# Layer 2's depthwise convolution on pairs of tokens: half the matmul passes, sixteen small spread transfers instead of four, and a gather behind them

## The chip, the cores and the metric

The kernel runs on the 8 cores of one Trainium2 chip. Each core has a tensor engine (PE, with its weight loads shown as PEld; it writes its results to a memory called PSUM), a vector engine (DVE), a scalar engine (ACT), GpSimd (POOL) and a sync engine (SP), which here does nothing but issue transfers. All transfers of a core run on its 16 DMA engines. The metric is the device time of the slowest core, in microseconds (us).

A program on all cores has a second, slower state, in which one die is granted a lower tensor clock.

Line numbers such as L921 are lines of that kernel's own source. Because the change inserts lines, the same work has other numbers afterwards:

| work in layer 2 | before | after |
|---|---|---|
| input projections (one helper for all layers) | L461 | L461 |
| gated product into G (DVE) | L882 | L893 |
| convolution (PE) | L921 | L937 |
| evacuation of the convolution, that is its copy out of PSUM, with bias (ACT) | L926 | L945 |
| square for the variance (ACT) | L928 | L958 |
| statistics (PE) | L937 | L966 |
| normalisation and SiLU (ACT) | L985 | L1015 |
| issue of any transfer (one helper) | L131 | L130 |

## The reference, cut to what matters

Four layers, one token mixer each. The change is in layer 2 alone, a Conformer convolution module: a gated product, a causal depthwise convolution with 31 taps over 2048 channels, a LayerNorm over the channels, SiLU.

```python
h = rms_norm(x, g_norm[i]) * (1.0 + scale) + shift
...
    a, ag, z = jnp.split(jnp.einsum('bsd,de->bse', h, w_in_c), 3, axis=-1)
    glu = a * jax.nn.sigmoid(ag)
    ext, conv_c_new = with_history(glu, hist_c, CCONV_W - 1)      # 30 earlier rows
    y = causal_depthwise_conv(ext, w_conv_c) + b_conv_c           # 31 taps, each channel for itself
    y = jax.nn.silu(layer_norm(y, ln_c_g, ln_c_b))                # statistics over all 2048 channels
    out = jnp.einsum('bse,ed->bsd', y * jax.nn.silu(z), w_out_c)
x = x + gate * out
```

Because the LayerNorm needs sums over all channels, nothing of the normalisation can start before the statistics of the last channel tile.

## The kernel before

Each core works on about 2 x 1,056 tokens in two groups (g = 0 and 1). In layer 2, 2048 channels make 16 tiles of 128, and a software-pipelined loop runs over them. In iteration i the tensor engine does the two projections of tile i, the convolution of tile i-2 and the statistics of tile i-3; the sync engine then spreads tile i:

```python
for i in range(16):
    ...                      # every second i: wait for the two weight tiles of i and i+1
    front(i, tl)             # 2 projections (PE), sigmoid (ACT), product into G (DVE)
    if i % 2 == 1:
        for sp in specs: release(sp)
        hook(i // 2)         # frees weight buffers; the next weight loads are issued by GpSimd
    if i >= 2: conv(i - 2)
    if i >= 3: stats(i - 3)
    spread(i)
zmm(0)                       # projections of the gate path z begin to be mixed in
conv(14); stats(13)
zmm(1)
conv(15); stats(14)
zmm(2)
stats(15)
variance()
...                          # then centre, normalise, multiply, limited largely by VectorE
```

A depthwise convolution has no sum over channels, so the kernel makes one for the tensor engine. Four transfers a tile copy G so that each block R[:, j] holds 32 channels at 4 token offsets: 128 rows. A weight matrix of 128 rows by 32 columns, zero except where row and column belong to the same channel, then applies 4 taps at once; 8 such passes (b) make 32 taps. Four blocks j run side by side on four column groups of the array.

```python
def spread(c):
    R, G = v3(tb(RB[ci], 4480), 4), tb(GB[ci], GW)
    for j in range(4):
        g = G[32 * j:32 * j + 32, CO:CO + RW]
        s.dma("sp", "gr%d_%d" % (ci, j), R[:, j, 0:RW],
              bass.AP(g.tensor, g.offset, [list(g.ap[0]), [1, 4], [1, RW]]), ...)
    ...                                           # DVE builds the masked weights wd

def conv(c):
    for b in range(8):
        for n in range(3):                        # 3 x 352 (or 362) tokens
            for j in range(4):                    # 4 column groups
                h.matmul(PSB[32*j:32*j+32, 3*sl + n, 0:WC], lhsT=wd[:, b, j, :],
                         rhs=R[:, j, 4*b + n*WC : 4*b + (n+1)*WC], start=(b == 0), stop=(b == 7), ...)
    ...                                           # ACT evacuates with the bias straight into ysT,
    ...                                           # then squares ysT into SQ
def stats(c):                                     # column sums of ysT and of SQ, accumulated over c
    ...
```

G, R, wd and SQ have two buffers each, chosen by the tile's parity.

## Time and profile before

The time before is 2298.93 us, the median of 3 runs (2295.59 to 2299.51). The profiled execution has a span of 2292.5 us.

| | kernel before |
|---|---|
| TensorE busy, share of the span | 2180.7 us, 95% |
| mean granted TensorE clock | 0.985 on the slowest core |
| one iteration of the channel loop | 11.47 us (group 0), 11.38 us (group 1) |
| of it: two projections / convolution / statistics | 7.47 / 3.71 / 0.29 us (group 0) |
| idle TensorE inside the loop | none |

These are lines of the profile page of the kernel before: busy time per engine, the chain of work that ended last (by engine, then by line), the group of the convolution, and the two kinds of spread transfer (size of each, median us from issue to landing).

```profile
PE 2180.7 (95%) x16875; PEld 1355.2 (59%) x16875; DVE 1046.1 (46%) x1482; ACT 638.4 (28%) x758; POOL 192.4 (8%) x336
...
PE 88%; DVE 5%; DMA 4%; ACT 2%; issue 1%; POOL 0%; DVEq 0%; SPq 0%; ACTq 0%; POOLq 0%
...
L921 PE MATMUL ps<-tmp 128*32 128x352 bf16 (+1 forms) x3072 | 122.9, 315 | 0.0
...
tmp<-tmp SPq DMA_DIRECT2D x64, 278.5 KB, 5.9
tmp<-tmp SPq DMA_DIRECT2D x64, 271.0 KB, 5.8
```

The number after the last bar of a group is the idle time of the engine just before its instructions: 0.0 for the convolution. It never waits.

This is the chain of waits of the kernel before in three iterations of the loop (start us, duration us, what):

```profile
1245.77 7.46 PE ps L461 x48
1253.24 3.71 PE ps L921 x96
1256.95 0.29 PE ps L937 x6
1257.24 7.47 PE ps L461 x48
1264.71 3.71 PE ps L921 x96
1268.42 0.29 PE ps L937 x6
1268.72 7.47 PE ps L461 x48
1276.18 3.71 PE ps L921 x96
```

Projections, convolution, statistics, then at once the next projections: the chain stays on the tensor engine. The convolution's 96 matmuls are 24 sets of four, so one set takes 3.71 / 24 = 155 ns.

This is the table by stretch for most of the same loop in the kernel before (busy us and instructions of each engine, granted clock, DMA share, GB/s):

```profile
1250.00:1385.00 135.00, 135.00 (x1785) 86.03 (x1783) 35.02 (x48) 38.61 (x36) 6.40 (x12) 1.00 0.64 145
```

The tensor engine is busy for all of 135 us at full clock; VectorE and ScalarE are busy for about a quarter.

### The profile page before, as it was taken

To read this page: it belongs to the slowest core of one execution; us is meant where nothing else is said; L and a number is where in the kernel's file an instruction comes from. 1 tells how busy PE (TensorE), PEld (TensorE's weight loads), DVE (VectorE), ACT (ScalarE), POOL (GpSimd) and SP (SyncE) were. 2 spreads that over 40 slices of the span, in tenths; PEclk is the share of its full clock that TensorE was granted. 3 is DMA by queue.
4 is the path that set the end of the run, shared out by engine and by line. 5 is a ranking of instruction groups with operands and counts; after the bars stand their busy time and mean duration, and the time that the engine had idled before them with its cause. 6 is when DMAs were issued, how large, how long until landed. Compare 5 with 4: busy or idle time off the path is not lost.

```text
span 2292.5 us, 41015 instructions; the slowest of 8 cores (2281.7 to 2292.5 us)
## 1 busy us (share of the span) xinstructions
PE 2180.7 (95%) x16875; PEld 1355.2 (59%) x16875; DVE 1046.1 (46%) x1482; ACT 638.4 (28%) x758; POOL 192.4 (8%) x336
## 2 busy tenths in 40 slices
PE   4999999998999999999999999999999999999996
PEld 1644656445666666666666666566666566666653
DVE  3454140542555454555544223753226566455535
ACT  2254312543011111111121224602335322303331
POOL 1012101111000000001000000100001000000000
PEclk9999999999999999999999999999999999999998
DMA  9906748057444634346446664537673534443423
GB/s 206 202 21 96 126 78 134 10 97 134 74 72 68 105 69 75 56 74 111 74 84 122 143 145 100 109 56 176 139 164 66 92 65 74 74 74 65 76 50 149
DMA packets 71030, 223.88 MB, mean 98 GB/s; under 512 B 9216, under 2 KB 9856, under 8 KB 70688
## 3 DMA queue, kind: packets, MB, share of 16 engines
q0 software_dynamic: 44928, 163.60, 42.6%
q1 hardware_dynamic: 25920, 57.68, 8.6%
q8 instruction: 136, 2.23, 0.4%
q14 instruction: 46, 0.38, 0.1%
HBM read 339.26 MB, written 9.55 MB: 152 GB/s over the span
## 4 chain that ended last, share of the span: by engine, by line
PE 88%; DVE 5%; DMA 4%; ACT 2%; issue 1%; POOL 0%; DVEq 0%; SPq 0%; ACTq 0%; POOLq 0%
PE ps L461 75%; PE ps L921 5%; PE ps L684 5%; DMA ring<-w_in_a 2%; DMA ring<-w_ada 1%; PE ps L753 1%; PE ps L749 1%; ACT hT L400 1%; DVE tmp L984 1%; DVE xb_sb L536 1%; DVE tmp L978 1%; DMA xa_sb<-xa 0%; DVE xa_sb L536 0%; PE ps L937 0%; PE ps L351 0%
## 5 line engine op out<-in xcount | busy, mean ns | idle before, releaser
L461 PE MATMUL ps<-hT,ring 128*128 128x352 bf16 (+1 forms) x8448 | 1300.8, 316 | 23.3 <-DVE ysT L760 5.7
L461 PEld LDWEIGHTS ps<-hT,ring 128*128 128x128 bf16 x8448 | 826.4, 98 | 489.8 <-issue 41.9
L461 PE MATMUL ps<-ysT,ring 128*128 128x352 bf16 (+1 forms) x3072 | 474.1, 315 | 16.7 <-DVE xb_sb L542 4.8
L461 PEld LDWEIGHTS ps<-ysT,ring 128*128 128x128 bf16 x3072 | 299.0, 98 | 191.8 <-issue 26.2
L882 DVE TENSOR_TENSOR tmp<-tmp,ps 128x1074 bf16<-128x1074 f32 (+3 forms) x64 | 45.4, 709 | 187.2 <-PE ps L461 183.9
L684 PE MATMUL ps<-ring,hT 128*128 128x512 bf16 (+1 forms) x576 | 127.1, 379 | 2.4 <-ACT ysT L649 1.3
L921 PE MATMUL ps<-tmp 128*32 128x352 bf16 (+1 forms) x3072 | 122.9, 315 | 0.0
L820 DVE TENSOR_TENSOR tmp<-tmp,ps 128x1074 f32<-128x1074 f32 (+3 forms) x64 | 45.4, 710 | 139.4 <-PE ps L461 136.1
L810 ACT ACTIVATE tmp<-ps 128x1074 f32<-128x1074 f32 (+1 forms) x32 | 33.9, 1058 | 261.9 <-PE ps L461 194.1
L921 PEld LDWEIGHTS ps<-tmp 128*32 128x32 bf16 x3072 | 80.1, 96 | 40.4 <-issue 9.4
L536 DVE SCALAR_TENSOR_TENSOR xb_sb<-ps,modT,xb_sb 128x1056 f32<-128x1056 f32 x32 | 42.1, 1316 | 128.7 <-PE ps L461 128.7
L536 DVE SCALAR_TENSOR_TENSOR xa_sb<-ps,modT,xa_sb 128x1074 f32<-128x1074 f32 (+1 forms) x32 | 42.1, 1326 | 123.7 <-PE ps L461 123.7
L926 ACT ACTIVATE ysT<-ps,cst_sb 128x1056 bf16<-128x1056 f32 (+3 forms) x64 | 44.8, 700 | 187.1 <-PE ps L921 184.1
L684 PEld LDWEIGHTS ps<-ring,hT 128*128 128x128 bf16 (+1 forms) x576 | 55.6, 98 | 67.4 <-issue 3.2
L837 DVE SCALAR_TENSOR_TENSOR tmp<-tmp,cst_sb 128x1074 f32<-128x1074 f32 (+1 forms) x64 | 85.1, 1329 | 6.7
L841 ACT ACTIVATE ysT<-ps 128x1074 bf16<-128x1074 f32 (+1 forms) x32 | 33.9, 1058 | 184.2 <-PE ps L461 184.2
L1084 ACT ACTIVATE tmp<-ps 128x1056 f32<-128x1056 f32 (+3 forms) x64 | 39.1, 611 | 156.9 <-PE ps L461 153.9
L771 DVE TENSOR_TENSOR ysT<-ysT,tmp 128x1074 bf16<-128x1074 bf16 (+1 forms) x32 | 22.8, 713 | 108.0 <-ACT tmp L770 108.0
L844 DVE TENSOR_TENSOR tmp<-tmp,ps 128x1074 f32<-128x1074 f32 (+3 forms) x64 | 45.4, 709 | 55.8 <-PE ps L461 52.4
L131 POOL DMA_DIRECT2D ring<-w_in_b x64 | 34.4, 538 | 386.0 <-PE ps L461 378.8
L760 DVE TENSOR_TENSOR ysT<-ps,ysT 128x512 bf16<-128x512 f32 (+2 forms) x72 | 44.1, 650 | 45.8 <-PE ps L753 45.5
L131 POOL DMA_DIRECT2D ring<-w_in_c x48 | 25.7, 538 | 459.7 <-PE ps L461 459.7
(154 smaller groups left out, 1628.7 us busy)
## 6 DMA issues: line engine op xcount, KB each, us to landing
ring<-w_in_b POOLq DMA_DIRECT2D x64, 512.0 KB, 5.7
ring<-w_ada POOLq DMA_DIRECT2D x48, 512.0 KB, 8.7
ring<-w_in_a POOLq DMA_DIRECT2D x48, 512.0 KB, 13.2
ring<-w_in_c POOLq DMA_DIRECT2D x48, 512.0 KB, 5.6
tmp<-tmp SPq DMA_DIRECT2D x64, 278.5 KB, 5.9
tmp<-tmp SPq DMA_DIRECT2D x64, 271.0 KB, 5.8
ring<-w_in_d POOLq DMA_DIRECT2D x32, 512.0 KB, 5.2
ring<-w_out_a POOLq DMA_DIRECT2D x16, 512.0 KB, 11.1
```

The costliest lines, as they stand in the source:

```text
L131: h.dma_start(out=out, in_=in_, **kw).then_inc(dsm, 16)
L461: ins = h.matmul(PSB[:, 3 * sl + n, 0:W], lhsT=lw, rhs=rh[:, n * W:(n + 1) * W], start=(first and k == 0), stop=(last and k == len(pairs) ...
L536: s.op("dve", lambda h, sl=sl, xv=xv, d=d: h.scalar_tensor_tensor(out=xv, in0=PSB[:, 3 * sl:3 * sl + 3, 0:W], scalar=gate[:, 16 + d, 0:1], ...
L684: ins = h.matmul(PSB[0:n, nq, :], lhsT=hT[:, kh * 4 + kk, hc:hc + n], rhs=vw[nq * 2 + kh][:, kk, :], start=(kh == 0 and kk == 0), stop=(kh ...
L760: s.op("dve", lambda h, bank=bank, y=y: h.tensor_tensor(out=y, in0=v3(PSB[:, 4 + bank, :], 4)[:, :, 0:no], in1=y, op=ALU.mult), reads=yk, ...
L820: s.op("dve", lambda h, ps=ps, cc=cc, n=n, nb=nb, smp=smp, p=p, CG=CG: h.tensor_tensor(out=shp(p[:, H + cc + smp * H:H + cc + smp * H + n] ...
L837: s.op("dve", lambda h, p=p, a=a, c=c, wd=wd, k=k: h.scalar_tensor_tensor(out=a[:, 0:wd], in0=p[:, k:k + wd], scalar=prmT[:, c, k:k + 1], ...
L844: s.op("dve", lambda h, ps=ps, cc=cc, n=n, nb=nb, smp=smp, a=a, CG=CG: h.tensor_tensor(out=shp(tf(CG + cc, n), nb), in0=shp(a[:, cc + smp ...
L882: s.op("dve", lambda h, ps=ps, cc=cc, n=n, nb=nb, smp=smp: h.tensor_tensor(out=shp(G[:, H + cc + smp * H:H + cc + smp * H + n], nb), in0=s ...
L921: ins = h.matmul(PSB[32 * j:32 * j + 32, 3 * sl + n, 0:WC], lhsT=wd[:, b, j, :], rhs=R[:, j, 4 * b + n * WC:4 * b + (n + 1) * WC], start=( ...
L926: s.op("act", lambda h, ps=ps, cc=cc, n=n, nb=nb: h.activation(out=shp(ysT[:, c, cc:cc + n], nb), in_=ps, func=AF.Identity, bias=prmT[:, c ...
L1084: s.op("act", lambda h, ps=ps, cc=cc, n=n, nb=nb, smp=smp, pv=pv: h.activation(out=shp(pv[:, H + cc + smp * H:H + cc + smp * H + n], nb), ...
```

## The change

The intent is to halve the convolution's tensor time. A row block now holds 16 channels x 2 token parities x 4 offsets, that is 8 offsets of 16 channels in 128 rows. One matmul of 128 rows to 32 columns makes 16 channels x 2 output tokens (even and odd). Each pass covers 8 taps instead of 4 and streams half the columns: 64 matmuls a tile, half of them only 176 or 191 wide, instead of 96 of 352 or 362. The price is in the layouts:

- the spread of a tile is 16 transfers of 64 rows (half as many rows, half as long) instead of 4 of 128 rows;
- the result comes out with two rows for a channel, so two new "gather" transfers a tile bring it back to one row for a channel;
- ScalarE evacuates in 4 or 6 pieces into a staging buffer; the square becomes a step of its own behind the gather and is done one iteration later, with one buffer instead of two;
- tokens are even-first from there on, and the normalisation restores the order by writing with a stride of two.

The diff, cut to its core (constants, host-side packing of the weights and bias, the writing of G in even-odd order and the end of the loop are left out; at the end, `conv(14)` now stands ahead of `zmm(0)` and `conv(15)` ahead of `stats(13)`, each with its gather behind it):

```diff
         def spread(c):
-            R = v3(tb(RB[ci], 4480), 4)
-            for j in range(4):
-                g = G[32 * j:32 * j + 32, CO:CO + RW]
-                s.dma("sp", "gr%d_%d" % (ci, j), R[:, j, 0:RW], ...)
+            R = v3(tb(RB[ci], 4480), 8)
+            for i in range(16):
+                j, r = i // 2, i % 2
+                g = G[16 * j:16 * j + 16, r * GH + CO // 2:r * GH + CO // 2 + RW]
+                s.dma("sp", "gr%d_%d" % (ci, i), R[64 * r:64 * r + 64, j, 0:RW], ...)
 ...
         def conv(c):
+            parts = [(0, 0, 0, n1, 0), (0, 1, 0, n2, n1), (1, 2, 0, n1, 0), (1, 1, n2, n2, n1)]
-                for b in range(8):
-                    for n in range(3):
+                for b in range(4):
+                    for hf, bank, at, n, m0 in parts:
                         for j in range(4):
 ...
+        def gather(c):
+            for hf in range(2):
+                s.dma("sp", "gy%d_%d" % (ci, hf), v3(ysT[64 * hf:64 * hf + 64, c, 0:NC], 2), Y[:, hf, :], ...)
+
+        def square(c):
+            s.op("act", ... activation(out=tb(SQ, NC), in_=ysT[:, c, 0:NC], func=AF.Square), ...)
 ...
         def norm(c):
-            s.op("act", ... activation(out=ysT[:, c, 0:NC], in_=t, func=AF.Silu, ...))
+            s.op("act", ... activation(out=ysT[:, c, 0:NC].rearrange("p (m r) -> p r m", r=2), in_=v3(t, 2), func=AF.Silu, ...))
 ...
+            if i >= 3:
+                square(i - 3)
             if i >= 2:
                 conv(i - 2)
             if i >= 3:
                 stats(i - 3)
             spread(i)
+            if i >= 2:
+                gather(i - 2)
```

Note where the gather stands: in program order, and so in the sync engine's queue, it comes after all 16 issues of spread(i).

## The prediction

> **What bounds the kernel now.** The page of the profile gives TensorE 95% of 2292.5 us, and the chain that ended last is 88% TensorE, 5.3% of it conv31. By groups, the conv's 3072 matmuls (128 rows to 32 columns, 352 or 362 wide) are busy 122.9 us. In the timeline of layer 2 one iteration of the channel loop takes 11.47 us (first token group) and 11.38 us (second), without a gap on TensorE: two input projections (7.47 us), conv of the tile two back (3.71/3.83 us), statistics (0.3 us). In the table by stretch TensorE is 100% busy there, VectorE 25%, ScalarE 29%, the DMA engines 65%.
>
> **What the change removes.** Four column groups run together: a set of four 352-wide matmuls takes 155 ns. Before: 8 x 3 sets a tile. After: 4 x (2 of 352 and 2 of 176-191), estimated 1.95-2.05 us by scaling with width. About 1.75 us less for each of 32 tiles: 56 us of TensorE time, all on the chain.
>
> **What it adds.** SyncE issues 16 spread transfers a tile instead of 4, and 2 gathers. In the sync engine's own records a spread issue takes at least 542 ns, and about 90 ns of wait and gap go with each: 633 ns. If that is per instruction and not per byte, SyncE needs 16 x 0.63 + 2 x 0.6 = 11.3 us a tile: more than the 9.7 us that TensorE would need, about what an iteration takes today. Bytes spread stay 1.1 MB, in descriptors half as long; a 1,920-byte packet takes 79 ns and a 960-byte one 44 ns, so the engines manage. ScalarE evacuates in 4 or 6 pieces instead of 1 or 3: estimated 0.8-1.3 us more a tile, with room.
>
> **How much is on the critical path.** The gather of a tile stands in SyncE's queue behind 16 issues of the next spread. Its statistics now wait for: conv end, 16 issues (about 10 us), two gather issues (1.2), landing (2-4), square on ScalarE (1.1). Then come statistics, projections and the conv that frees the other buffer: about 24 us around for two tiles, so 12 us or more an iteration, against 11.47 now and 9.7 by TensorE alone. Weight loads make it worse: in the packet records two prefetched weight tiles filled the engines for about 6 us, and spread transfers issued meanwhile moved nothing for 4 us. The Trainium skill, "DMA: Bandwidth & Descriptors", section "Issuing engines are not separate DMA queues", says that all share the same 16 engines; this trace agrees. So I expect alternate iterations of about 11 and 14 us, the tensor gain swallowed, and 15 to 30 us lost in each token group; TensorE idle just before the statistics matmuls.
>
> **Predicted: 2345 us**, 8 in 10 within 2280 to 2405. Faster by over 2%: 0.08; within 2%: 0.43; slower by over 2%: 0.49.
>
> **What would show each step.** Conv busy about 62-66 us in the groups. Spread issues near 540 ns each in SyncE's records (right), near 300 (wrong). Waits: the statistics' TensorE line waiting for ScalarE's square, that for the gather; 2-5 us an iteration. Loop iterations averaging 12-13 us. Outside layer 2's channel loop nothing moves by more than a few us.
>
> **What would make it wrong.** An issue of 64 descriptors at 350 ns or less with its wait: then iterations near 10 us and a gain of 25-45 us. The other way: idle stretches of 4 us or more, after which the clock is granted lower (the Trainium skill, "TensorE: Matmul & The Clock Gate", Part 1; in the table by stretch the clock was 0.94 where TensorE had a long gap), or 176-wide sets bound by their weight loads.

## The result, and the profile after

The kernel after takes 2464.36 us (median of 4 fast runs, 2463.65 to 2468.47), against 2297.26 us for the kernel before (4 fast runs, 2294.99 to 2299.51). The ratio is 1.073 (95% interval 1.071 to 1.075): slower by 7.3%, 167 us. Ratios here and below are the mean time of one kernel's fast runs over that of the other's in the same rounds, so not quite the ratio of the medians that I quote. Executions in which one die ran at a lower clock are left out of the means. The profiled execution was a fast one, with a span of 2463.4 us.

Slower was the likeliest of my three cases, but 2464 us lies well outside the range of 2280 to 2405 us.

The lines of the profile page of the kernel after that answer to those shown of before:

```profile
PE 2168.1 (88%) x15834; PEld 1335.2 (54%) x15851; DVE 1045.8 (42%) x1482; ACT 671.0 (27%) x854; POOL 191.8 (8%) x337
...
PE 72%; SPq 8%; DMA 7%; DVE 5%; issue 3%; ACT 3%; DVEq 0%; POOL 0%; ACTq 0%; POOLq 0%
...
L966 PE MATMUL ps<-ysT,onesE 128*32 128x352 bf16 x96 | 12.5, 380 | 169.1 <-ACT tmp L958 169.1
...
L958 ACT ACTIVATE tmp<-ysT 128x1056 bf16<-128x1056 bf16 x32 | 34.6, 1080 | 210.4 <-DMA ysT<-tmp 210.4
...
L937 PE MATMUL ps<-tmp 128*32 128x352 bf16 (+2 forms) x2048 | 70.5, 294 | 9.7 <-DMA tmp<-tmp 7.4
...
tmp<-tmp SPq DMA_DIRECT2D x256, 69.4 KB, 2.9
tmp<-tmp SPq DMA_DIRECT2D x256, 67.5 KB, 3.1
...
ysT<-tmp SPq DMA_DIRECT2D x64, 132.0 KB, 3.1
```

The convolution itself got what was promised: 122.9 us became 70.5 us. But 169.1 us of idle tensor time now stand just before the statistics (L966), which wait for the square on ScalarE, and the square waits for the gather (ysT<-tmp). The sync engine's queue (SPq) and DMA, together 4% of the chain before, are 15% of it. The 169.1 us of idle time and the 167 us of loss are alike by chance: tensor work was also saved, and the clock fell.

The table by stretch of the kernel after, for the stretch shown of before:

```profile
1250.00:1385.00 135.00, 88.04 (x949) 52.73 (x948) 22.50 (x33) 32.59 (x50) 4.27 (x8) 0.82 0.63 117
```

The tensor engine is now busy for 88 of 135 us, and the clock granted is 0.82. The waits of the kernel after in this stretch (total us, times, longest us) say where:

```profile
ACT tmp L958 <- DMA ysT<-tmp: 62.0, 7, 15.5
...
PE ps L966 <- ACT tmp L958: 45.3, 4, 12.3
```

Four waits of about 11 us in 135 us: one for every second iteration. The chain of waits of the kernel after shows one full turn of two iterations. I leave out all but the first and the last of the 16 spread issues, VectorE's 16 semaphore waits ahead of its product (1347.41 to 1348.51, shown as "issue"), and single pieces of about 0.05 us.

```profile
1336.73 0.78 PE ps L966 x6
1337.51 9.85 PE ps L461 x48
...
1348.55 1.28 DVE tmp L893
...
1349.93 0.25 DVE tmp L897
...
1350.35 0.59 SPq L130
...
1361.14 0.55 SPq L130
1361.77 0.58 SPq L130
1362.35 0.05 issue
1362.40 6.67 DMA ysT<-tmp
1369.15 1.09 ACT tmp L958
1370.24 0.14 issue
1370.38 0.78 PE ps L966 x6
```

From one late statistics to the next it is 1370.38 - 1336.73 = 33.65 us, or 16.8 us an iteration, against 11.47 before. (The twelve turns of the two groups take 32.1 to 34.6 us.) Its parts, as differences of the starts above:

| part of the turn | us |
|---|---|
| statistics, then two projections | 0.78 + 9.85 |
| end of projections to first spread issue (product on VectorE lies here) | 2.99 |
| 16 spread issues on the sync engine | 11.42 |
| first gather issue | 0.63 |
| second gather, from its issue to landing | 6.67 |
| square, with the gaps around it | 1.31 |

Why only every second iteration? The stall of about 11 us gives the following tile's gather time to land, so the next statistics find it ready. In the timeline those statistics start at 1349.10 after the convolution, without such a wait; then the turn begins again.

The loss is in the loop. These marks, in us from the first layer-2 projection of a group, were read from the tensor engine's records:

| | group | statistics of tile 12 begin | statistics of tile 15 end | output projections begin |
|---|---|---|---|---|
| before | 0 | 175.4 | 195.3 | 247.3 |
| before | 1 | 173.8 | 193.9 | 245.9 |
| after | 0 | 253.8 | 278.6 | 334.2 |
| after | 1 | 248.1 | 273.5 | 328.7 |

The two groups lose 87 and 83 us up to the output projections, which is all of the 167 us within the scatter of cores and runs. The stretch between the last statistics and the output projections grew from 52.0 us to 55.6 (group 0) and 55.1 us (group 1).

### The profile page after: what moved, and what is told of

It reads as the page before. It is cut to its first block, busy times and chain, and to the rows that moved or that the text cites. A ratio compares the mean times of both kernels' runs of the same rounds, so it can differ in the third digit from the quotient of the medians.

```text
span 2463.4 us, 40921 instructions; the slowest of 8 cores (2445.3 to 2463.4 us)
## 1 busy us (share of the span) xinstructions
PE 2168.1 (88%) x15834; PEld 1335.2 (54%) x15851; DVE 1045.8 (42%) x1482; ACT 671.0 (27%) x854; POOL 191.8 (8%) x337
## 4 chain that ended last, share of the span: by engine, by line
PE 72%; SPq 8%; DMA 7%; DVE 5%; issue 3%; ACT 3%; DVEq 0%; POOL 0%; ACTq 0%; POOLq 0%
PE ps L461 65%; SPq L130 8%; PE ps L684 5%; DMA ysT<-tmp 4%; DMA ring<-w_in_a 1%; DMA ring<-w_ada 1%; DVE tmp L893 1%; ACT tmp L958 1%; PE ps L753 1%; PE ps L749 1%; ACT hT L400 1%; DVE xb_sb L536 1%; PE ps L966 1%; DVE tmp L1007 1%; DMA xa_sb<-xa 0%
## 5 line engine op out<-in xcount | busy, mean ns | idle before, releaser
L461 PE MATMUL ps<-hT,ring 128*128 128x352 bf16 (+1 forms) x8448 | 1331.1, 320 | 25.9 <-DVE ysT L760 5.7
L461 PEld LDWEIGHTS ps<-hT,ring 128*128 128x128 bf16 x8448 | 836.7, 100 | 516.7 <-issue 48.7
L966 PE MATMUL ps<-ysT,onesE 128*32 128x352 bf16 x96 | 12.5, 380 | 169.1 <-ACT tmp L958 169.1
L966 PEld LDWEIGHTS ps<-ysT,onesE 128*32 128x32 bf16 x96 | 3.9, 98 | 175.1 <-issue 174.6
L958 ACT ACTIVATE tmp<-ysT 128x1056 bf16<-128x1056 bf16 x32 | 34.6, 1080 | 210.4 <-DMA ysT<-tmp 210.4
L945 ACT ACTIVATE tmp<-ps,cst_sb 128x16 bf16<-128x16 f32 (+2 forms) x160 | 69.7, 435 | 72.5 <-PE ps L937 57.2
L937 PE MATMUL ps<-tmp 128*32 128x352 bf16 (+2 forms) x2048 | 70.5, 294 | 9.7 <-DMA tmp<-tmp 7.4
```

The costliest lines, as they stand in the source:

```text
L461: ins = h.matmul(PSB[:, 3 * sl + n, 0:W], lhsT=lw, rhs=rh[:, n * W:(n + 1) * W], start=(first and k == 0), stop=(last and k == len(pairs) ...
L937: ins = h.matmul(PSB[32 * j:32 * j + 32, 3 * sl + bank, at:at + n], lhsT=wd[:, 4 * hf + j, b, :], rhs=R[:, 4 * hf + j, 4 * b + m0:4 * b + ...
L945: s.op("act", lambda h, hf=hf, bank=bank, at=at, o=o, k=k, d=d: h.activation(out=Y[:, hf, d:d + k], in_=PSB[:, 3 * sl + bank, at + o:at + ...
L958: s.op("act", lambda h: h.activation(out=tb(SQ, NC), in_=ysT[:, c, 0:NC], func=AF.Square), reads=["ys.%d" % c, "ysh0.%d" % c, "ysh1.%d" % ...
L966: ins = h.matmul(PSB[32 * q:32 * q + 32, b, 0:W], lhsT=onesE, rhs=src[:, q * W:(q + 1) * W], start=(c == 0), stop=(c == 15), skip_group_ch ...
```

## The experiments

The trace suggests two limits and two aggravations, and they can be told apart:

- **Latency.** The statistics sit only one iteration behind the gather, and the gather sits behind 16 issues. If only this counted, using the result one iteration later would bring the loop to the tensor engine's own pace of about 9.7 us.
- **Throughput of the sync engine.** 16 issues, one every 0.63 us at best, and two gather issues are over 11 us a tile, whoever waits. If this is the limit, a later consumer helps only down to that pace, and a second issuing engine is needed.
- **Weight loads.** GpSimd issues two loads of 512 KB every second iteration, at 1358.04 us in the turn above. They fill the DMA engines while the gather waits to land.
- **The clock.** After an idle stretch the same 48 projection matmuls took 9.85 us instead of 7.47.

### e1: use the gather one iteration later

```diff
-            if i >= 3:
-                square(i - 3)
+            if i >= 4:
+                square(i - 4)
             if i >= 2:
                 conv(i - 2)
-            if i >= 3:
-                stats(i - 3)
+            if i >= 4:
+                stats(i - 4)
```

with square(12) and stats(12) added after the loop.

> The changed kernel, with the square and the statistics of a tile consumed one iteration later; nothing is issued differently. Theory A (latency): TensorE stands still because the gather waits in SyncE's queue behind 16 spread issues and then lands late; a later consumer hides it, TensorE sets the pace at 9.7 us an iteration, total 2250 to 2275 us. Theory B (throughput): SyncE cannot issue 18 transfers in an iteration; the loop is then paced by SyncE at 11.5 to 12.6 us, total 2320 to 2350 us, and TensorE waits for spread transfers in the conv instead of for the square. Under both the granted clock in the loop is back over 0.95.

Measured: 2382.78 us, ratio 1.036 (1.033 to 1.039), results correct; 82 us better than the change, still 84 us worse than before. The statistics' long waits are gone. In their place the convolution waits for the spread, as the waits of this run in the same stretch show:

```profile
PE ps L937 <- DMA tmp<-tmp: 21.1, 8, 4.0
```

and the chain of waits has moved to the sync engine. Its summary for 27 us of this run, and two of its lines:

```profile
by line: SPq L130 86.9%; issue 12.1%; SPq L129 2.5%
...
1339.96 0.54 SPq L130
1340.59 0.54 SPq L130
```

The sync engine issues one transfer after the other, most of them one every 0.63 us, and now and then one that takes longer (1.64 us at 1333.55). From the statistics of tile 0 to those of tile 12, twelve iterations, it never pauses for more than 0.5 us in either group; in the change its pauses in the same stretch add up to 45 and 40 us. These iterations take 12.75 (group 0) and 13.18 us (group 1) on average, that is 18 issues at 0.71 to 0.73 us each. So using the gather later takes half of the loss away, and what is left is set by the sync engine's throughput. The kind of limit was as the throughput theory expected; pace and total were both somewhat above its ranges (11.5 to 12.6 and 2320 to 2350 us).

### e2: gather before spread in the queue

```diff
-            spread(i)
             if i >= 2:
                 gather(i - 2)
+            spread(i)
```

> The changed kernel, with the gather of tile i-2 placed ahead of the spread of tile i in SyncE's queue. Theory A (order in the queue makes the latency): the statistics no longer wait for 16 issues, the idle time of TensorE before them falls from 11 us in every second iteration to under 3 us, total 2300 to 2350 us; what is left is SyncE's throughput plus its wait for ScalarE's evacuation, 12 to 14 us an iteration. Rival C (landing of the gather in contention with the weight loads is the greater part): the gather still lands 6 to 7 us after its issue in every second iteration and the total stays over 2400 us.

Measured: 2385.96 us, ratio 1.038 (1.035 to 1.041), correct. It does the same thing from the other side: the gather no longer stands behind 16 issues, the statistics stop waiting, and the convolution waits for the spread instead (18.7 us in 6 waits in the same stretch). That two quite different cures of the latency end within 4 us of each other is what a limit behind both of them would give, and here too the sync engine hardly pauses in the twelve iterations (1.1 and 0.5 us in all, at 13.0 and 13.1 us an iteration). The total that I had expected here was too low.

### e3: no weight loads during the loop (wrong results on purpose)

```diff
-            s.dma("pool", "rs%d" % i, ring[...], w_dram[spec[0]][spec[1]], ...)
+            if spec[0] != "in2" or spec[1] in (0, 8):
+                s.dma("pool", "rs%d" % i, ring[...], w_dram[spec[0]][spec[1]], ...)
```

Layer 2 then computes with stale weights; the output is wrong, the work on every engine but GpSimd, which issues the loads, and the DMA engines is the same.

> The changed kernel without the loads of layer 2's input weights but the first two tiles of each group; wrong results on purpose. It takes the weight traffic out of the channel loop and leaves the order of issue. Rival C (weights delay the gather): issue to landing of the gather falls from 6.7 us to 2.5-3 us, every second statistics wait from 11 us to about 7 us, total about 60 us shorter (7 stalls of about 4 us in each of two groups): 2395 to 2415 us. If the weights do not matter the total stays within 15 us of 2464.

Measured: 2409.14 us (one run), 55 us better than the change. The chain of waits of this run, one turn, with the issues left out (lines are one higher here, so L967 is the statistics and L462 the projections):

```profile
1330.13 0.78 PE ps L967 x6
1330.90 8.93 PE ps L462 x48
...
1354.53 3.02 DMA ysT<-tmp
1357.63 1.09 ACT tmp L959
1358.72 0.14 issue
1358.86 0.77 PE ps L967 x5
```

The waited-for gather lands in 3.02 us instead of 6.67, and the turn is 28.73 us instead of 33.65. So more than half of the gather's landing time was spent beside, or behind, the weights. Alternate iterations still differ (12.6 and 16.8 us on average in group 0), so it is not the loads, which come in every second iteration, that make the alternation. The expectation held.

### e4 and e8: keep the tensor clock up with dummy matmuls

Before the waiting statistics, in every second iteration, e4 adds 70 matmuls of 32 columns (256 wide), and e8 adds 125 of the full 128 columns (160 wide). Both write to a part of PSUM that nobody reads.

```diff
+                if i % 2 == 1:
+                    warm(70)            # e8: warm(125), full array
                 stats(i - 3)
```

> The changed kernel with 70 dummy matmuls into an unused corner of a bank (about 7.5 us) ahead of the statistics in every second iteration, to keep TensorE active while it waits. Theory D (the clock drops in the 11 us stalls and stretches the two projections after them from 7.5 to 9.9 us): those take 7.5 us again, the granted clock in the loop rises from 0.82 to over 0.95, total 25 to 40 us shorter: 2425 to 2440 us. If the clock does not matter to the loop, the total stays within 10 us of 2464.

> Second try on the clock: the changed kernel with 125 dummy matmuls that use all 128 columns (160 wide, about 9 to 10 us) in the stalls of every second iteration; the first try used 32 columns, left 3 to 5 us idle and did not bring the clock back. Theory D: the projections after the stall take 7.5 us again and not 9 to 10 us, and the total falls by 25 to 40 us, to 2425 to 2440 us. If the projections go back to 7.5 us and the total does not move, the loop is closed by the transfers and not by TensorE's pace.

e4 measured 2465.17 us in one run. The projections after the stall still took 8.4 to 10.0 us in all but one of the twelve turns (7.33 there). It left 3 to 5 us of idle time before the statistics, so it does not separate the two readings and is inconclusive.

e8 measured 2451.53 us in its only run, a fast one: 13 us better than the change, where 25 to 40 were expected, a miss. In seven of twelve turns it kept the clock. The timeline of the tensor engine in this run (start us, busy us, operation; in brackets the idle time before):

```profile
1309.33 0.33 PE L966 MATMUL ps<-ysT,onesE 128*32 128x352 bf16 x3 [2.45 <-ACT tmp L958]
...
1309.74 7.54 PE L461 MATMUL ps<-hT,ring 128*128 128x358 bf16 x48
...
1329.28 8.82 PE L977 MATMUL ps<-sc 128*128 128x160 bf16 x125
1341.13 0.33 PE L966 MATMUL ps<-ysT,onesE 128*32 128x352 bf16 x3 [3.04 <-ACT tmp L958]
...
1341.54 7.53 PE L461 MATMUL ps<-hT,ring 128*128 128x358 bf16 x48
```

Here the projections after the stall take 7.53 us, and this turn is 1341.13 - 1309.33 = 31.80 us. In the other five turns of the same run the projections still took 8.9 to 10.0 us. The seven turns with kept projections take 30.5 to 32.1 us, the five others 32.1 to 34.0 us. So the clock is part of the loss: between 1 and 2 us a turn where it was kept. Its share in the whole is shown only in part, and by one run.

### e5: e1, with the gathers issued by ScalarE

```diff
-                s.dma("sp", "gy%d_%d" % (ci, hf), ...)
+                s.dma("act", "gy%d_%d" % (ci, hf), ...)
```

> The statistics consumed one iteration later (as in the first experiment), and the gathers issued from ScalarE's queue instead of SyncE's, right behind the evacuation. SyncE is left with 16 issues a tile. Theory B (SyncE's issue time paces the loop: 18 issues took about 12.6 us an iteration there): two issues fewer, 10.3 to 11.4 us an iteration, total 2330 to 2360 us. If the pace came from the engines that move the bytes, it stays at 12.6 us and the total at about 2380 us.

Measured: 2354.25 and 2355.33 us, ratio 1.026 (1.023 to 1.028), correct. Taking two of 18 issues from the sync engine saves 28 us against e1. The loop's pace of 12.15 and 12.39 us over the same twelve iterations (e1: 12.75 and 13.18) was not as good as I expected (10.3 to 11.4): the spread issues themselves took 0.65 us on average, so 16 of them with their gaps are still above the tensor engine's pace. The total was in the range.

### e12: only the second issuing engine, without the later use

```diff
-                s.dma("sp", "gr%d_%d" % (ci, i), ...)
+                s.dma("pool" if i % 2 else "sp", "gr%d_%d" % (ci, i), ...)
```

> The changed kernel with every second spread issued from GpSimd's queue, and the statistics consumed where the change has them. Completes a square: 2464 us with neither, 2383 us with late statistics, about 2285 us with both. If only SyncE's issue throughput mattered, this alone would give about 2285 us. If the latency of the gather matters beside it: behind 8 issues and not 16 the gather comes 5 us earlier, so the stall before every second iteration's statistics falls from 11 us to 3 to 6 us, total 2330 to 2380 us.

Measured: 2369.73 us, ratio 1.031 (1.029 to 1.033), correct; 95 us better than the change. The waits of this run in the same stretch:

```profile
PE ps L966 <- ACT tmp L958: 22.6, 6, 5.9
```

Half the waiting time of the change (45.3 us), still at the statistics: the issues before the gather are fewer, the order is the old one. The chain of waits is the turn of the change made shorter: from the first spread issue to the first gather issue it takes 6.82 us (1355.37 to 1362.19) in place of 11.42. So this run, too, gains by a shorter turn; the sync engine still pauses for 60 and 44 us in the twelve iterations. The expectation held.

### e6: both, the later use and the second issuing engine

The edits of e1 and e12 together.

> The statistics consumed one iteration later, and every second spread issued from GpSimd's queue: SyncE has 8 spreads and 2 gathers, about 6.5 us, GpSimd 8 spreads beside its weight loads. Bytes and descriptors stay as they are. Theory B: no queue is longer than TensorE's 9.7 us, the loop runs at 9.7 to 10.2 us an iteration, total 2250 to 2290 us. Rival E (the 16 DMA engines, at 65 to 70% now, or landing in contention, set the pace): 11.5 us an iteration or more, total over 2330 us. A GpSimd issue that costs over 1 us would also hold it back, which the trace will show.

Measured: 2284.34, 2284.52 and 2289.98 us in three runs, ratio 0.996 (0.994 to 0.998), correct. This is 180 us better than the change, and 0.4% better than the kernel before. The four corners make a square:

| median, us | statistics at i-3 | statistics at i-4 |
|---|---|---|
| all 16 spreads on the sync engine | 2464 (change) | 2383 (e1) |
| 8 of them on GpSimd | 2370 (e12) | 2285 (e6) |

The two cures are worth 82 and 95 us alone and 180 us together, so neither contains the other, and both are needed. That is the main finding. It is no split of the loss into two separate halves: in the change itself the turn alone set the pace, and e12 gains by shortening it. Using the gather later takes the turn away and leaves the issue rate as the limit (e1); with 8 of the 18 issues elsewhere the sync engine has time to spare again (pauses of 21 and 4 us in the twelve iterations of e6).

The table by stretch for 80 us of the loop in this run:

```profile
1300.00:1380.00 80.00, 75.63 (x982) 48.43 (x979) 22.80 (x32) 31.40 (x48) 35.15 (x70) 1.00 0.89 187
```

The clock is back at 1.00; GpSimd (the fifth engine) is now busy for 44% of the time with issues. One iteration in this run's timeline:

```profile
1316.04 7.52 PE L461 MATMUL ps<-hT,ring 128*128 128x358 bf16 x48 [0.41 <-DVE tmp L893]
1323.49 1.99 PE L937 MATMUL ps<-tmp 128*32 128x352 bf16 x64
1325.31 0.32 PE L966 MATMUL ps<-ysT,onesE 128*32 128x352 bf16 x3
1325.46 0.32 PE L966 MATMUL ps<-tmp,onesE 128*32 128x352 bf16 x3
1326.19 7.52 PE L461 MATMUL ps<-hT,ring 128*128 128x358 bf16 x48 [0.41 <-DVE tmp L893]
```

10.15 us an iteration: projections 7.52, convolution 1.99, statistics, and 0.41 us of idle time that VectorE's product causes (it first passes 16 semaphore waits, one for each transfer). This is the loop that the change was meant to give.

Why is the whole then only 0.4% faster, when the convolution alone saves over 50 us? The same marks as above answer for group 0:

| | statistics of tile 12 begin | statistics of tile 15 end | output projections begin |
|---|---|---|---|
| before | 175.4 | 195.3 | 247.3 |
| e6 | 165.9 | 188.2 | 243.5 |

The tensor saving should be 16 x 1.72 = 27.5 us a group. Of it 9.5 us are left when the statistics of tile 12 begin, 7.1 us when the last ones end, and 3.8 us at the output projections. In the trace of e6 I find: 12 waits of the projections for VectorE's product, 5.6 us in all, in the loop; three waits of 5.45, 1.67 and 3.2 us at the end of the loop, where the last gathers land and no projections of further tiles are left to hide them; slowed projections after these waits (5.98 and 5.38 us for 24 matmuls that take 3.69 us otherwise); and 3 us in the stretch after the statistics. Together that is about 23 of the 24 us that are missing. In group 1, 7.2 us of the saving are left at the output projections (238.7 against 245.9). The two groups keep 11 us, and the runs are 10 us faster.

### e7, e9, e10, e11: harvesting the rest

Each builds on e6. e7 restores the token order in VectorE's operations, so that ScalarE need not write with a stride:

```diff
-            activation(out=ysT[:, c, 0:NC].rearrange("p (m r) -> p r m", r=2), in_=v3(t, 2), func=AF.Silu, ...)
+            activation(out=ysT[:, c, 0:NC], in_=t, func=AF.Silu, ...)     # DVE's center and mult reorder instead
```

> As the run before, and the tokens are put back in order when VectorE subtracts the mean (32-bit output) instead of when ScalarE writes the normalised tile as 16-bit elements with a stride of two. In the changed kernel that ScalarE write takes 1.58 us for 1.26 us before, and the stretch from the last statistics to the output projection is 3.6 us longer in each group. Expected: the ScalarE write is back at 1.26 us, VectorE's two operations stay at 1.25 us, total 4 to 8 us below the run before. If VectorE pays for the stride, they grow and the total is not lower.

Measured: 2284.80 us as the median of four fast runs, ratio 0.995 (0.993 to 0.997). ScalarE's write fell back from 1576 to 1263 ns and VectorE's operations stayed at 1257 and 1272 ns. The expected 4 to 8 us did not come, a miss: the time is that of e6 (2284.52 us) within the scatter, so the length of that write does not set the pace there.

e9 mixes the projections of the gate path in earlier at the end of the loop:

```diff
+        zmm(0)
         square(12); conv(14); gather(14); stats(12)
-        zmm(0)
+        zmm(1)
         square(13); conv(15); gather(15); stats(13)
+        zmm(2)
         square(14)
-        zmm(1)
         stats(14)
-        zmm(2)
+        zmm(3)
```

> The sixth experiment's kernel (statistics one iteration later, every second spread from GpSimd's queue) with the end of the channel loop rearranged: a gate projection is put ahead of each of the last convs and statistics, so that TensorE has work while the last spreads and gathers land. In the sixth experiment the loop took 10.1 us an iteration but TensorE stood 5.5, 1.7 and 3.2 us in the tail, with slow projections after them. Expected: from the last loop statistics to the output projection 5 to 10 us less in each group, total 2265 to 2280 us. If the stretch after the statistics (limited by VectorE, about 52 us) takes it back, the total stays at 2284 us.

Measured: 2280.26 to 2283.26 us in the three fast runs, ratio 0.994 (0.992 to 0.997). This is above the 2265 to 2280 us that I expected.

e10 adds to e9 a tiny memset on G in group 0, early in the iteration, so that VectorE passes its 16 waits before the projections end:

```diff
+            if g == 0 and c >= 2:
+                s.op("dve", lambda h: h.memset(G[:, GH - 2:GH], 0.0), writes=gk)
```

> As the run before, and VectorE collects its waits for the 16 spread transfers that read the buffer earlier: a memset of two unused columns, which needs nothing from TensorE, stands ahead of the product. In the sixth experiment 16 waits of 69 ns each stood between the end of the projection and the product, and TensorE then waited 0.41 us an iteration for the product to free its bank. Expected: that wait is gone in the first group's loop (in the second two copies already stand ahead), 9.7 us an iteration, total 4 to 8 us below the run before.

Measured: 2281.40 us as the median of the four fast runs (2271.54 to 2284.77 us), ratio 0.993 (0.990 to 0.996); the total moved by less than the 4 to 8 us that I expected. The gap of 0.41 us is gone in group 0 and an iteration takes 9.68 us there. At the end of the loop the tensor engine waits 6.05, 1.22, 3.20 and 2.26 us, more than in e6: a faster loop arrives earlier at the same landing times.

e11 keeps e10's memset and orders the end of the loop differently again (convolutions of tiles 14 and 15 first, statistics of 12 to 15 after):

```diff
         zmm(0)
-        square(12)
         conv(14); gather(14)
-        stats(12)
         zmm(1)
-        square(13)
+        square(12)
         conv(15); gather(15)
-        stats(13)
+        stats(12)
         zmm(2)
+        square(13); stats(13)
+        zmm(3)
         square(14); stats(14)
-        zmm(3)
```

> As the tenth experiment, where the loop ran at 9.7 us an iteration but the tail took it back: the statistics of tile 12 stood right behind the loop and waited 6.0 us for its gather, those of 13 to 15 waited 1.2, 3.2 and 2.3 us, and two gate projections ran at a lower clock after it. Here the last convs and two gate projections come first and the four statistics later. Expected: the last statistics end 10 to 16 us earlier in each group than in the tenth experiment, total 2255 to 2272 us, about 1.0 to 1.8% below the kernel before. If VectorE, which needs about 52 us after the last statistics, is not the limit there, it can be less by another few us.

Measured: 2288.58 us, ratio 0.995 (0.994 to 0.997), against an expected 2255 to 2272: a miss. Now conv(15) waits 4.48 us for the last spread, whose transfers took 7.76 us to land. The wait moves about; none of these orders removes it.

e6, e7, e9, e10 and e11 can't be told apart by their intervals. The best point value is e10's, 0.7% faster than before. How the rest could be had stays open.

## Why the prediction was wrong

**What bounds the kernel before:** right. The loop had no gap on the tensor engine.

**What the change removes:** right. I estimated 1.95 to 2.05 us for a convolution; 1.99 us (group 0) and 2.04 us (group 1) were measured, and the convolution's group went from 122.9 to 70.5 us, a little above the "62-66" that I gave.

**Cost of an issue:** right in kind. A spread of 64 short rows takes at least 544 ns to issue, one of 128 long rows took at least 542 ns: between these two shapes it is per instruction, not per byte. The mean was 626 ns, since 50 of the 512 issues took over 800 ns; no run shows why. With the gaps between them, 16 issues took 11.42 us in the turn shown, where I had put "about 10 us". There is luck in this: I used the least time, while the 128 spread issues of the kernel before take 1029 ns on average, and I gave no reason why the shorter transfers should stay near the least.

**The critical path:** right in its order but for where the spread starts, wrong in its size. This is the step that failed, as the prediction put it: "about 24 us around for two tiles, so 12 us or more an iteration". The turn is 33.65 us. Adding up my own terms with the middle of "2-4" for the landing gives 25.1 us. Term by term:

| term of the turn | predicted, us | measured, us | difference |
|---|---|---|---|
| two gather issues and landing | 1.2 + 2-4 | 0.63 + 6.67 | +3.1 |
| projections | 7.5 | 9.85 | +2.4 |
| 16 spread issues | 10 | 11.42 | +1.4 |
| from projections to the first issue | 2.0 (as the convolution) | 2.99 | +1.0 |
| statistics, square | 0.3 + 1.1 | 0.78 + 1.31 | +0.7 |
| sum | 25.1 | 33.65 | +8.6 |

- The *landing* was mis-sized most. I had written that weight loads fill the engines for about 6 us and "make it worse", and then put 2 to 4 us in the sum. e3 settles it: without the loads the landing is 3.02 us and the whole 55 us shorter. In group 0 of the change, the gathers that the statistics wait for land in 6.7 to 7.3 us from the second turn on, the others in about 3.1.
- The *clock* was the second. I named the low clock after idle stretches of 4 us as something that would make the prediction wrong, and left it out of the sum, although stalls in alternate iterations were my own forecast. The Trainium skill, "TensorE: Matmul & The Clock Gate", Part 1, says that the array falls to half clock after an idle window of about 3.4 us and needs about as long of work to recover. The trace agrees on the half clock: just before the turn shown the tensor engine falls idle at 1325.9 us and works again from 1336.7, and the granted clock is 0.50 from 1328.7 to 1342.4 us and 1.00 from there to 1362.8; the projections that start at 1337.51 take 9.85 us, and the mean over the loop is 0.82. On the length of the window it agrees only roughly: in e8, projections of 9.19 us followed idle stretches of only 2.61 and 2.77 us. e8 shows the link, where the clock was kept.
- The *path itself* began in the wrong place. The spread does not follow the convolution but the product on VectorE. That starts 1.2 us after the projections end, because VectorE passes 16 semaphore waits at 69 ns each, one for each spread transfer; the product is 1.28 us more. The 16 transfers thus cost twice, once at issue and once at the wait.
- I expected idle stretches of "2-5 us an iteration". They are about 11 us in every second one, since slow and fast iterations alternate. I had "about 11 and 14 us" for the two kinds; the pair takes 33.65 us, not 25.

**"Outside layer 2's channel loop nothing moves by more than a few us":** right. The normalisation's strided write went from 1262 to 1576 ns, and the stretch behind the statistics grew by 3.6 us in group 0 and 3.2 in group 1. e7 shows that the write's own duration was not critical.

**Was the sync engine busy all the time?** I argued from its throughput ("11.3 us a tile") and from the latency together. In the change it was idle from 1342.2 to 1350.3 us in the turn shown: latency alone set the pace. e1 brought the throughput limit to light, and the square of e1, e12 and e6 shows that each cure alone leaves about half of the loss. I said that a tile's issues take "11.3 us", "about what an iteration takes today". As a floor that was right, if low: e1's loop stands at 12.75 and 13.18 us.

The Trainium skill, "DMA: Bandwidth & Descriptors", "Rules for kernel authors", says that spreading transfers over several issuing engines does not help bandwidth and only saves sequencer time. No run here tests the bandwidth; the saving, 8 issues fewer ahead of each gather, was worth 95 us (e12). The page "Perfetto Trace Analysis" has the better pointer, in "What 'DMA-bound' means" and in "DMA Optimizations": one form of being DMA-bound is an issuing sequencer full of transfer slices, and then balancing over the issuing engines may help. The chain of e1, 86.9% sync-engine issues, is that picture, and e6 the cure.

## What to carry to other kernels

When a change replaces a few big on-chip transfers by many small ones, multiply the number of issues by the measured time of one, and compare that with the iteration it has to fit in: here 18 x 0.63 us against 9.7 us (in e1 it was 0.71 to 0.73 us each, with the slow issues counted). Then write down the turn through every engine, with each term read from the trace under the load it will meet (the landing beside weight loads, the projections after an idle stretch), and not as it is when all is quiet. A result that comes back by a transfer should be used a whole iteration later than seems needed, and a queue should not put the transfer that somebody waits for behind those that nobody waits for yet; but do not expect such a cure to help beyond the pace of the engine that issues.

## What the Trainium skill lacked or had wrong

- "DMA: Bandwidth & Descriptors" has no issue time by shape for transfers from the sync engine (only one count of cycles for earlier generations, in a comparison with trn3); its table for the GpSimd path gives about 50 ns for dispatch and calls descriptor generation small. The runs show 542 ns at least for a spread of 128 rows of 2,168 bytes and 544 ns at least for 64 rows of 1,080 bytes, 532 ns for a gather of 64 x 2 runs of 1,056 bytes, and 332 ns for a plain store of 128 rows of the result (before and after alike). Between two issues lie about 90 ns, with the semaphore wait in them.
- The same page, "Issuing engines are not separate DMA queues", calls the issue time "usually small relative to the DMA itself". Here it was not: one transfer landed in about 3 us, but issues of one engine follow each other while landings overlap, and 16 issues took 11.42 us.
- No page that I read gives the time of an issue that is held up. 50 of 512 spread issues took over 800 ns, up to 1.8 us, instead of 544; what held them is not shown.
- GpSimd issued the same spread transfer in 500 ns by the profile, whose spans on GpSimd are rough, with little scatter (500 to 598 ns), beside a sync engine whose issues then averaged 789 ns (e6). I found no such figure for trn2 in the pages that I read.
- No page that I read prices a semaphore wait on VectorE's sequencer (one gives a time for reading a semaphore's value, which is not the same): 69 ns each here, 1.1 us for 16.
- "DMA: Bandwidth & Descriptors" tells that all issuing engines share the 16 DMA engines, but not what a small on-chip transfer waits beside two loads of 512 KB: 6.67 us to land instead of 3.02 (e3).
